# A dilated convolution on one core: the seventh pair's second image stored over 112 and four times 4 partitions, the last pair's first halves stored in one transfer

## The chip, the core and the metric

The kernel runs on one core of one Trainium2 chip. The metric is the device time of the program in microseconds; the lower the better. Three runs of the kernel before took 126.48, 126.51 and 126.69 us, the median is 126.51 us. One more execution was taken with the hardware profiler. It took 126.59 us, of which 124.8 us lie between the first and the last instruction (the span); all positions below are counted from the span's start.

## What is computed

A 3x3 convolution with dilation 2 and padding 2, in float32, of 16 images of 64 channels and 64x64 pixels into 16 images of 128 channels and 64x64 pixels:

```python
for b, co, ci, kh, kw:
    output[b, co] += weight[co, ci, kh, kw] * x_pad[b, ci, 2*kh:2*kh+64, 2*kw:2*kw+64]
```

The inputs are 16.8 MB of images and 0.3 MB of weights, the output is 33.6 MB. All of it crosses between HBM and SBUF once.

## The kernel before, in words

The 16 images are worked on as 8 pairs (`pb` 0 to 7). A pair's two images of 64 channels fill the 128 partitions of the input tile `x32`. A pair is cut into 4 groups of 16 image rows (`g` 0 to 3, `GR = 16`), so there are 32 groups `G`, written out in one Python loop. The instruction order on each engine is the order of the program text (`manual_schedule`).

For each group ScalarE casts the input to float16 (`cast`, line 73), VectorE adds neighbouring rows of it (`rowsum`, line 85), TensorE makes three PSUM tiles `psP`, `psA` and `psB` (line 171), ScalarE copies `psP` to SBUF (line 233), and VectorE adds it to `psA` and `psB` and writes the sums into the output tile `osb` (line 240). Casts run several groups ahead of the matmuls.

The output tile `osb` of a pair has 128 partitions (the output channels) of 8192 float32 each: 4096 of the pair's first image (16 KB), then 4096 of the second. There are three such tiles in rotation, and three of the float32 input tiles.

All transfers are issued by SyncE (SP), in program order: `load` (line 64) brings a pair's input in, `store` (line 185) takes one image's rows `r0` to `r1` of one output tile out, over the partition ranges in `rows`, and `store_both` (line 191) takes the same rows of both images in one transfer. Eight completion semaphores are used in turn, so a transfer is issued only after the one eight places before it has landed; a load also waits until its tile has been cast, and a store until VectorE has written what it reads. A DMA engine works through its share of the transfers in the order of their issue.

In the order of issue the part that matters here is: the load of pair 7 (`load(7, (0, 32, 64))`, two transfers of 32 rows, 8 KB a partition each), issued when pair 3 is done; then two stores of 2 MB for each of pairs 3 to 6, each image whole, 16 KB a partition. Pair 7 is the last. After its second group four transfers go out:

```python
store(pb, 0, 0, 2 * GR)                          # image 0, 32 rows, 8 KB a partition
store(pb, 1, 0, 2 * GR - ROWS4)                  # image 1, 24 rows, 6 KB a partition
store(pb, 1, 2 * GR - ROWS4, 2 * GR, FOUR)       # image 1, 8 rows: partitions 0-123, then 124-127
```

and after its fourth group the second halves, two transfers of 32 rows. The split at partition 124 matters because of how a transfer is shared out: in the trace a transfer over 128 partitions raises its completion semaphore sixteen times, once for each of the 16 DMA engines, and each engine has eight rows of it, whereas the transfer over 124 partitions raised it four times from engines, and the packet records show four engines with 31 rows of 2 KB each; the transfer over the last 4 partitions gave the same four engines one row each.

Of the kernel before, what the change touches and what calls it, by code (L numbers as in the profile page):

```python
# [10 lines left out]
def kernel(  # L11
# [9 lines left out]
    B, CI, H, W = x.shape  # L21
# [7 lines left out]
    P = 128  # L29
# [6 lines left out]
    GR = 16  # L36
# [3 lines left out]
    npairs = B // 2  # L40
    ngroups = npairs * NG
    chunk_rows = [(g * GR + (d if g else 0), min((g + 1) * GR + d, H)) for g in range(NG)]
    XF = 3
# [17 lines left out]
    def load(pb, cuts=(0, H)):  # L61
        x32_tiles[pb] = fpool.tile([P, HW], f32, tag="x32", name="x32")
        for lo, hi in zip(cuts[:-1], cuts[1:]):
            nc.sync.dma_start(  # L64
                out=x32_tiles[pb][:, lo * W : hi * W], in_=x_pair[pb, :, lo * W : hi * W]
            )
# [10 lines left out]
    def rowsum(c):  # L77
        pb, g = divmod(c, NG)
        if g == 0:
            xs_tiles[pb] = sxpool.tile([P, HW // 2], f16, tag="xs", name="xs")  # L80
        v = x16_tiles[pb][:, g * GR * W : (g + 1) * GR * W].rearrange(
            "p (b e q) -> p b e q", e=2, q=2 * W
        )
        s = xs_tiles[pb][:, g * NH : (g + 1) * NH].rearrange("p (b q) -> p b q", q=2 * W)
        nc.vector.tensor_tensor(out=s, in0=v[:, :, 0], in1=v[:, :, 1], op=add)  # L85
# [67 lines left out]
    def casts(G):  # L153
        for n in range(2 if G else 3):
            c = ahead[0]
            if c >= ngroups or c > G + (7 if c < 2 * NG else 5):
                return
            cast(c)
            ahead[0] += 1

    def product(ps, src, kind, blk0, nblk, first, last):
        for j in (1, 0, 2):
            dw = (j - 1) * d
            o0, o1 = max(0, -dw), W - max(0, dw)
            t = kind * KW + j
            for hb in range(2):
                pp = slice(hb * CI, (hb + 1) * CI)
                rhs = src(pp, dw + o0, dw + o1)
                po = ps[:, hb * NH + blk0 * 2 * W : hb * NH + (blk0 + nblk) * 2 * W]
                po = po.rearrange("p (r w) -> p r w", w=W)[:, :, o0:o1]  # L170
                nc.tensor.matmul(  # L171
                    out=po,
                    lhsT=w_sb[pp, t * CO : (t + 1) * CO],
                    rhs=rhs,
                    start=first and j == 1,
                    stop=last and j == 2,
                )

    def blocks(x16, b0, n, e):
        v = x16.rearrange("p (b e r w) -> p b e r w", e=2, r=2, w=W)  # L180
        return lambda pp, c0, c1: v[pp, b0 : b0 + n, e, :, c0:c1]

    def store(pb, m, r0=0, r1=H, rows=((0, P),)):
        for lo, hi in rows:
            nc.sync.dma_start(
                out=out_img[2 * pb + m, lo:hi, r0 * W : r1 * W],
                in_=o_tiles[pb][lo:hi, m * HW + r0 * W : m * HW + r1 * W],
            )

    def store_both(pb, r0, r1):  # L190
        nc.sync.dma_start(
            out=out_img[2 * pb : 2 * pb + 2, :, r0 * W : r1 * W].rearrange("m o q -> o m q"),
            in_=o_tiles[pb].rearrange("p (m q) -> p m q", m=2)[:, :, r0 * W : r1 * W],
        )

    FOUR = ((0, P - 4), (P - 4, P))
    ROWS4 = 8

    for G in range(ngroups):
        pb, g = divmod(G, NG)  # L200
        x16 = x16_tiles[pb]
        xs = xs_tiles[pb].rearrange("p (r w) -> p r w", w=W)
        if g == 0:
            o_tiles[pb] = opool.tile([P, 2 * HW], f32, tag="osb", name="osb")
        o = o_tiles[pb].rearrange("p (m b e q) -> p m b e q", m=2, e=2, q=2 * W)
        b0 = g * NBLK

        def summed():
            ps = ppool.tile([P, 2 * NH], f32, tag="p", name="psP")
            sv = lambda pp, c0, c1: xs[pp, g * GR // 2 : (g + 1) * GR // 2, c0:c1]  # L210
            product(ps, sv, 0, 0, NBLK, True, True)
            return ps

        if G:
            psP = summed()

        psA = apool.tile([P, 2 * NH], f32, tag="ab", name="psA")
        product(psA, blocks(x16, b0, NBLK, 1), 1, 0, NBLK, True, False)
        z = 1 if g == 0 else 0
        product(psA, blocks(x16, b0 + z - 1, NBLK - z, 1), 2, z, NBLK - z, False, True)  # L220

        psB = apool.tile([P, 2 * NH], f32, tag="ab", name="psB")
        product(psB, blocks(x16, b0, NBLK, 0), 3, 0, NBLK, True, False)
        z = 1 if g == NG - 1 else 0
        product(psB, blocks(x16, b0 + 1, NBLK - z, 0), 4, 0, NBLK - z, False, True)

        if not G:
            psP = summed()

        if not G:  # L230
            casts(0)
        p_sb = spool.tile([P, 2 * NH], f32, tag="psb", name="p_sb")
        nc.scalar.copy(out=p_sb, in_=psP)  # L233
        if G:
            casts(G)
        if G + 1 < ngroups:
            rowsum(G + 1)
        pv = p_sb.rearrange("p (m b q) -> p m b q", m=2, q=2 * W)
        for e, ps in ((0, psA), (1, psB)):
            nc.vector.tensor_tensor(  # L240
                out=o[:, :, b0 : b0 + NBLK, e],
                in0=ps.rearrange("p (m b q) -> p m b q", m=2, q=2 * W),
                in1=pv,
                op=add,
            )

        if G == 0:
            load(XF)
        if g == NG - 1 and 0 < pb < npairs - XF - 1:
            load(pb + XF + 1, (0, H) if pb < 3 else (0, H // 2, H))  # L250
        if G == NG - 2:
            store(0, 0, 0, (NG - 1) * GR)
            store(0, 1, 0, (NG - 1) * GR)
        if G == NG - 1:
            store_both(0, (NG - 1) * GR, H)
            load(XF + 1)
        elif pb == npairs - 1:
            if g % 2 == 1:
                store(pb, 0, (g - 1) * GR, (g + 1) * GR)
                if g == 1:  # L260
                    store(pb, 1, 0, 2 * GR - ROWS4)
                    store(pb, 1, 2 * GR - ROWS4, 2 * GR, FOUR)
                else:
                    store(pb, 1, (g - 1) * GR, (g + 1) * GR)
        elif g == NG - 1:
            store(pb, 0)
            store(pb, 1)

# [34 lines left out]
```

## Time and profile before

| what | value |
|---|---|
| median of three runs | 126.51 us (126.48 to 126.69) |
| profiled execution | 126.59 us |
| its span | 124.8 us |
| TensorE busy | 105.2 us, 84% of the span |
| VectorE busy | 91.0 us, 73% |
| ScalarE busy | 64.9 us, 52% |
| DMA moved | 50.78 MB, mean 407 GB/s |
| last VectorE instruction ends | 109.5 us |
| last store issued | 109.94 us |
| last store landed | 123.98 us |

A busy TensorE row counts pipelined matmuls, so 84% is not a distance to its peak. The DMA row counts the share of time in which the 16 DMA engines had a packet; packets of one engine overlap by 3 or 4 ns in the records, so that a wholly busy engine shows 1.01 to 1.02. The position of each packet, its duration and its size stand in the trace's packet records, and the moments at which a transfer's semaphore was raised in its semaphore records.

### The profile page before, as it was taken

To read this page: it belongs to the slowest core of one execution; us is meant where nothing else is said; L and a number is where in the kernel's file an instruction comes from. 1 tells how busy PE (TensorE), PEld (TensorE's weight loads), DVE (VectorE), ACT (ScalarE), POOL (GpSimd) and SP (SyncE) were. 2 spreads that over 40 slices of the span, in tenths; PEclk is the share of its full clock that TensorE was granted. 3 is DMA by queue.
4 is the path that set the end of the run, shared out by engine and by line. 5 is a ranking of instruction groups with operands and counts; after the bars stand their busy time and mean duration, and the time that the engine had idled before them with its cause. 6 is when DMAs were issued, how large, how long until landed. Compare 5 with 4: busy or idle time off the path is not lost.

```text
span 124.8 us, 2343 instructions
## 1 busy us (share of the span) xinstructions
PE 105.2 (84%) x1002; PEld 56.9 (46%) x1002; DVE 91.0 (73%) x103; ACT 64.9 (52%) x68; POOL 2.3 (2%) x8
## 2 busy tenths in 40 slices
PE   6985999999999999999999999999999999600000
PEld 2342555555555555555555555555555555300000
DVE  0661998988898889888988898889888988700000
ACT  4368897665666566656665666566653333200000
POOL 2400000000000000000000000000000000000000
PEclk9999999999999999999999999999999999965555
DMA  5999999999999999999999999999999999999981
GB/s 142 356 437 446 431 420 441 360 429 402 457 432 425 425 415 436 438 431 399 420 441 412 415 441 431 441 420 425 431 425 425 425 436 431 431 412 414 428 374 74
DMA packets 4594, 50.78 MB, mean 407 GB/s; under 512 B 488, under 2 KB 488, under 8 KB 1256
## 3 DMA queue, kind: packets, MB, share of 16 engines
q1 hardware_dynamic: 4584, 50.63, 96.5%
q8 instruction: 8, 0.13, 0.4%
q14 instruction: 2, 0.02, 0.0%
HBM read 17.07 MB, written 33.55 MB: 406 GB/s over the span
## 4 chain that ended last, share of the span: by engine, by line
PE 76%; DMA 6%; ACT 2%; DVE 1%; DVEq 1%; SPq 1%; issue 0%
PE psA L171 31%; PE psB L171 30%; PE psP L171 16%; DMA x<-in_x_dram 6%; ACT x L73 2%; DVE osb L240 1%; DVEq L300 1%; ACT p_sb L233 1%; SPq L64 0%; SPq L88 0%; DVEq L240 0%
## 5 line engine op out<-in xcount | busy, mean ns | idle before, releaser
L171 PEld LDWEIGHTS <-w_sb 64*128 64x128 f16 x960 | 54.6, 94 | 46.4 <-issue 1.6
L233 ACT COPY p_sb<-psP 128x1024 f32<-128x1024 f32 x32 | 32.4, 1013 | 36.8 <-issue 21.5
L240 DVE TENSOR_TENSOR osb<-psA,p_sb 128x1024 f32<-128x1024 f32 x32 | 39.2, 1225 | 13.5 <-PE psA L171 9.8
L171 PE MATMUL psA<-x,w_sb 64*128 64x496 f16 (+3 forms) x384 | 45.1, 365 | 0.5 <-ACT x L146 0.5
L171 PE MATMUL psB<-x,w_sb 64*128 64x496 f16 (+3 forms) x384 | 45.1, 365 | 0.0
L240 DVE TENSOR_TENSOR osb<-psB,p_sb 128x1024 f32<-128x1024 f32 x32 | 39.1, 1222 | 0.0
L73 ACT CAST x<-x 128x1024 f16<-128x1024 f32 (+2 forms) x31 | 32.1, 1045 | 0.6 <-DMA x<-in_x_dram 0.6
L171 PE MATMUL psP<-xs,w_sb 64*128 64x496 f16 (+1 forms) x192 | 26.0, 371 | 1.3 <-ACT p_sb L233 1.3
L85 DVE TENSOR_TENSOR xs<-x 128x512 f16<-128x512 f16 x32 | 13.3, 416 | 0.7 <-ACT x L73 0.7
L101 PE MATMUL dm<-zero 128*128 128x512 f16 x12 | 4.9, 539 | 1.2 <-DVE zero L93 1.2
L101 PEld LDWEIGHTS <-zero 128*128 128x128 f16 x12 | 1.3, 126 | 3.1 <-issue 1.7
L111 DVE CAST wd<-w 128x192 f16<-128x192 f32 x1 | 0.5, 505 | 2.4 <-DMA w<-in_weight_dram 2.4
L113 ACT ACT_TABLE_LOAD x1 | 1.3, 1283 | 0.7 <-PEq L286 0.7
L124 PEld LDWEIGHTS <-wd 128*64 128x64 f16 x30 | 0.9, 109 | 1.4 <-DVE wd L111 0.7
L124 PE MATMUL wt<-ident,wd 128*64 128x128 f16 x30 | 1.4, 224 | 0.0
L136 ACT CAST w_sb<-wt 128x384 f16<-128x384 f32 x1 | 0.5, 480 | 1.7 <-PE wt L124 1.7
L113 ACT CAST wd<-w 128x192 f16<-128x192 f32 x1 | 0.5, 542 | 1.5 <-DMA w<-in_weight_dram 1.5
L146 ACT CAST x<-x 128x512 f16<-128x512 f32 x1 | 0.6, 620 | 0.6 <-DMA x<-in_x_dram 0.6
L93 DVE MEMSET zero<- 128x256 uint32 x1 | 0.3, 272 | 0.9 <-PEq L286 0.9
L138 DVE CAST w_sb<-wt 128x384 f16<-128x384 f32 x1 | 0.6, 558 | 0.4 <-PE wt L124 0.4
L112 POOL TENSOR_TENSOR wd<-w 128x192 f16<-128x192 f32 x1 | 0.8, 797 | 2.3 <-DMA w<-in_weight_dram 2.3
L115 POOL CAST wd<-w 128x192 f16<-128x192 f32 x1 | 0.8, 810 | 0.0
(11 smaller groups left out, 3.8 us busy)
## 6 DMA issues: line engine op xcount, KB each, us to landing
out_dram<-osb SPq DMA_DIRECT2D x12, 2048.0 KB, 18.1
x<-in_x_dram SPq DMA_DIRECT2D x6, 2048.0 KB, 14.8
out_dram<-osb SPq DMA_DIRECT2D x4, 1024.0 KB, 13.1
out_dram<-osb SPq DMA_DIRECT2D x2, 1536.0 KB, 11.3
x<-in_x_dram SPq DMA_DIRECT2D x2, 1024.0 KB, 19.0
x<-in_x_dram SPq DMA_DIRECT2D x1, 1088.0 KB, 5.7
x<-in_x_dram SPq DMA_DIRECT2D x1, 960.0 KB, 7.5
out_dram<-osb SPq DMA_DIRECT2D x1, 768.0 KB, 15.2
```

What stands on the lines that cost most here:

```text
L73: nc.scalar.copy(out=x16_tiles[pb][:, lo * W : hi * W], in_=x32_tiles[pb][:, lo * W : hi * W])
L85: nc.vector.tensor_tensor(out=s, in0=v[:, :, 0], in1=v[:, :, 1], op=add)
L101: nc.tensor.matmul(out=dm[:, 0:512], lhsT=zero[:, 0:P], rhs=zero)
L112: nc.gpsimd.tensor_tensor(out=wdv[:, 3], in0=wv[:, 0], in1=wv[:, 1], op=sub)
L113: nc.scalar.copy(out=wdv[:, 2], in_=wv[:, 0])
L115: nc.gpsimd.tensor_copy(out=wdv[:, 4], in_=wv[:, 2])
L124: nc.tensor.matmul(out=wts[k % 3][r * CI : (r + 1) * CI, c0 + j * CO : c0 + (j + 1) * CO], lhsT=wd[:, t * CI : (t + 1) * CI], rhs=ident,)
L138: nc.vector.tensor_copy(out=t2[0], in_=t2[1])
L171: nc.tensor.matmul(out=po, lhsT=w_sb[pp, t * CO : (t + 1) * CO], rhs=rhs, start=first and j == 1, stop=last and j == 2,)
L233: nc.scalar.copy(out=p_sb, in_=psP)
L240: nc.vector.tensor_tensor(out=o[:, :, b0 : b0 + NBLK, e], in0=ps.rearrange("p (m b q) -> p m b q", m=2, q=2 * W), in1=pv, op=add,)
L300: with _tile.TileContext(nc) as tc:
```

## The change

Three edits, all of transfers that SP issues:

- The load of pair 7 is one transfer of 2 MB, 16 KB a partition, as the other pairs' loads are; it was two of 1 MB.
- The second image of pair 6 was stored in one transfer over 128 partitions; it is now stored in five: one over partitions 0 to 111 and four over 4 partitions each (112-115 to 124-127), rows of 16 KB in all of them.
- The first halves of pair 7's two images were stored in four transfers (32 rows of image 0; 24 rows of image 1; 8 rows of image 1 over 124 and over 4 partitions). They are now stored by one transfer of both images, with two runs of 8 KB for each partition.

The second halves of pair 7 are stored as before. No instruction of TensorE, VectorE, ScalarE or GpSimd is added, removed or moved. SP issues 32 transfers in all, as before.

```diff
-    FOUR = ((0, P - 4), (P - 4, P))
-    ROWS4 = 8
+    LOW = P - 16
+    FOURS = ((0, LOW),) + tuple((lo, lo + 4) for lo in range(LOW, P, 4))
...
-            load(pb + XF + 1, (0, H) if pb < 3 else (0, H // 2, H))
+            load(pb + XF + 1)
...
-            if g % 2 == 1:
-                store(pb, 0, (g - 1) * GR, (g + 1) * GR)
-                if g == 1:
-                    store(pb, 1, 0, 2 * GR - ROWS4)
-                    store(pb, 1, 2 * GR - ROWS4, 2 * GR, FOUR)
-                else:
-                    store(pb, 1, (g - 1) * GR, (g + 1) * GR)
+            if g == 1:
+                store_both(pb, 0, 2 * GR)
+            elif g == 3:
+                store(pb, 0, 2 * GR, H)
+                store(pb, 1, 2 * GR, H)
         elif g == NG - 1:
             store(pb, 0)
-            store(pb, 1)
+            store(pb, 1, rows=FOURS if pb == npairs - 2 else ((0, P),))
```

## The prediction

> **What bounds the kernel now.** I read the page's slices and queues first, then what SP waits for, then the last microseconds in narrow stretches, then SP's and ScalarE's order of time. On the page:
>
> ```profile
> DVE  0661998988898889888988898889888988700000
> DMA  5999999999999999999999999999999999999981
> q1 hardware_dynamic: 4584, 50.63, 96.5%
> q8 instruction: 8, 0.13, 0.4%
> ```
>
> The DMA row is full from the second slice to the last but one, while VectorE, the last engine to work, stops at 109.5 us. The page's chain ends on compute and does not follow the DMA, so its 76% of TensorE is not what sets the end. SP's waits after 100 us say what does:
>
> ```profile
> SPq L300 <- DMA out_dram<-osb: 13.0, 3, 8.3
> ```
>
> At the end of the program SP waits 13 us for stores alone. Whether the engines have work throughout is read in stretches (columns: stretch, its length, granted clock, DMA share, GB/s):
>
> ```profile
> 60.00:72.00 12.00, 1.00 1.01 427
> ...
> 96.00:108.00 12.00, 1.00 1.01 430
> 108.00:120.00 12.00, 0.59 1.00 419
> 120.00:124.80 4.80, 0.50 0.39 164
> ```
>
> A share of 1.01 is all sixteen engines without a gap. The packet records agree: nearly every packet starts 3 or 4 ns before the one before it on its engine ends. So the kernel is bound by the DMA engines, each with its own list of packets, and its end is the end of the engine that finishes last. How unevenly they finish, in stretches as long as one 8 KB packet takes:
>
> ```profile
> 119.98:120.29 0.31, 0.50 0.95 402
> 120.59:120.90 0.31, 0.50 0.76 321
> 121.20:121.51 0.31, 0.50 0.58 241
> 121.82:122.12 0.31, 0.50 0.51 214
> 122.43:122.73 0.31, 0.50 0.26 107
> 122.73:123.04 0.31, 0.50 0.25 107
> 123.04:123.35 0.31, 0.50 0.13 54
> ```
>
> One engine is 27 GB/s: fifteen are at work at 120.1, nine at 121.4, four at 122.9; in the last row two packets start, and the later one ends last. Following the packets back engine by engine, the last ends are 123.65, 123.35, 123.29 and 123.26. The first two of these four are engines that had the 2 KB rows (of which the other two end at 122.50 and 122.58); call the latest of these **d**. The ends at 123.29 and 123.26 are two other engines, call them the **slow pair**; the remaining ten end between 120.05 and 122.2. Landing is seen 0.33 us behind d's last packet (123.98), and the span ends 0.8 us later.
>
> **The change part by part.** The price of a packet is its duration less the overlap, from the packet records: 16 KB 611 - 4 = 607 ns, 8 KB 309 - 3 = 306, 6 KB 234 - 3.5 = 230.5, 2 KB 84 - 4 = 80, and 9 - 3 = 6 for the 4-byte packet that raises a semaphore.
>
> How 112 rows are shared out, no row shows. 128 rows went to sixteen engines, 124 and 4 rows to four; each time the number of engines divides the rows. 112 is 16 x 7, so I take sixteen engines with seven rows each; the far end, four engines as with 124 rows, is a rival below.
>
> The four engines that d belongs to, before: load of pair 7 16 x 306 = 4896; second image of pair 6 8 x 607 = 4856; then 8 x 306 = 2448, 8 x 230.5 = 1844 and 32 x 80 = 2560; together 16604 ns and 7 semaphore packets. After: load 8 x 607 = 4856; pair 6 (7 + 4) x 607 = 6677; both first halves 16 x 306 = 4896; together 16429 ns and again 7 semaphore packets. Saved: **175 ns**. In bytes nothing moves: they had 62 + 2 KB of small rows for a fair share of 16 KB, 48 KB too many; now they have 4 x 16 KB less the one row of 16 KB that they lose, 48 KB too many again. The gain is only that 64 KB travel in 4 packets for 32.
>
> The other twelve, the slow pair among them, before: 4896 + 4856 + 2448 + 1844 = 14044 and 5 semaphore packets; after: 4856 + 7 x 607 + 4896 = 14001 and 3. Saved: 43 + 12 = **55 ns**.
>
> So d ends at 123.65 - 0.175 = 123.47, the slow pair at 123.29 - 0.055 = 123.23: d still ends last, and the gain is d's 0.175 us. Were d quicker still, the slow pair would cap the gain at 123.65 - 123.23 = 0.42 us.
>
> What is costed at nothing, and its cover:
>
> ```profile
> 55.09 1.20 SPq L64 DMA_DIRECT2D x<-in_x_dram  x2
> 97.17 0.97 SPq L185 DMA_DIRECT2D out_dram<-osb  x2
> 103.27 2.34 SPq L185 DMA_DIRECT2D out_dram<-osb  x4
> 109.54 1.03 SPq L185 DMA_DIRECT2D out_dram<-osb  x2
> 82.03 1.16 ACT L73 CAST x<-x 128x1152 f16<-128x1152 f32 x1
> ```
>
> The whole load lets pair 7's first cast (82.03 us, the last row, from ScalarE's timeline) wait for all of it; the two halves had landed at 73.04 and 75.49, so 6.5 us of cover are left. Four more issues behind 97.17, at 0.6 us each (2.34 / 4), end by 101, before the next store can be issued at 103.27; three issues fewer there leave SP idle, which costs nothing. An issue also waits for the transfer eight places before it. The places move between the load of pair 7 and the small stores; the tightest is now the very last store, which comes to stand behind the first image of pair 6 (landed 109.67, while this store was issued at 109.94). The four small ones stand behind stores of pairs 3 and 4, landed by 95.0. The earliest engine would run dry only at some 115 us (its end 120.05 less two shares of 2.45), 5 us behind the last issue. VectorE's wait for the store of pair 3, 0.3 us at 85.4, is covered likewise, since VectorE is 14 us ahead of the end.
>
> [...]
>
> **The sum.** Against the profiled execution's own time: 126.59 - 0.175 = 126.42 us. That execution stood 0.08 us above the median of 126.51, so on the median 126.34 us, 0.14% less. A measurement of this kernel tells about 0.2%, 0.25 us, from no change.
>
> **The rivals.**
>
> *The instruction fetches fall on other engines.* The eight packets of q8 are 16 KB each, one about every 13 us, each on another engine, which they hold back by one packet, 607 ns. In the packet records the one at 81.04 fell on d and those at 16.11 and 95.10 on the slow pair: three of the four latest engines have had one each. If another list of transfers moves them, d ends at 122.87 and the slow pair sets 123.23: -0.42, 126.09 us. If one falls on the other late engine of the four (123.35), it ends at 123.35 - 0.175 + 0.607 = 123.78, +0.13: 126.64. Against it: the instructions fetched are TensorE's and they don't change, and the three runs lie within 0.21 us, so in the kernel before the places seem to be fixed.
>
> *The four engines get in each other's way* (slower). In each 4-row transfer four engines read four neighbouring partitions in packets of 607 ns. d's neighbours run 0.3 us and about 1.1 us ahead of it, so half of each of its packets overlaps the next engine's. If two such readers halve each other's rate, d's four packets grow by up to 0.3 us each: +1.2 - 0.175, 127.5 us. It decides over the forecast from 44 ns a packet on, where the gain is used up. Against it: the 2 KB rows, read by four engines beside twelve others, took 84 ns every single time. But those were 31 partitions apart, and the four neighbouring rows of the old kernel hardly met: they were 84 ns long and started at 117.52, 117.59, 118.36 and 118.66.
>
> *Small transfers hold their engines.* If each of the four must land before its engine goes on (0.33 us as at the end), d gains 4 x 0.33 = 1.3 us: 127.7. Against it: behind the 124-row transfer the next row started at once, at 117.516 behind a semaphore packet at 117.510. [...]
>
> *The 112 rows are not spread over sixteen engines.* Over four: 28 rows each for 7, 21 x 607 = 12.7 us, 139 us. Over fourteen with eight rows each, as every engine has of 128: d has one row more, +0.61 - 0.175 = +0.43, 126.94 us.
>
> **How the numbers follow.** The forecast, 126.34, has 0.62: with the scatter of the runs (0.1 each way) and the engines' stalls on the early loads its own range is 126.15 to 126.55; 0.13 of it lies below 126.26, which is 0.25 under the median, 0.47 within, 0.02 above. The fetches moved: 0.22, of which 0.17 faster, 0.03 within and 0.02 slower by over 0.2%. Neighbours in the way 0.09, small transfers held 0.03, 112 rows otherwise 0.04: all slower. Faster 0.13 + 0.17 = 0.30; within 0.2% 0.47 + 0.03 = 0.50; slower 0.02 + 0.02 + 0.16 = 0.20. The range runs from the fetches' best, 126.09, with a little scatter, to 126.75, which takes in the fetches' worst and a tenth of scatter; left out are the three slower rivals, 0.16.
>
> **What the profile after would show.** Packets of 112 rows on sixteen engines, 7 each, and 16 KB packets of 611 ns in the four small transfers; if these take 650 or more, neighbours are in the way. The 2 KB and 6 KB packets gone. The last packet's end at 123.47 on one of the four engines. The same eight fetches on the same engines; d without one would show as an end set by two engines that had no small transfers. DMA share 1.01 until 120. I am wrong if the last stretches show one or more of the four engines alone for over half a microsecond, or if a load's stalls, which set the engines apart by up to 1 us in the first 25 us, come out otherwise.

## The result, and the profile after

The changed kernel is slower: ratio 1.0229 to the kernel before, 95% interval 1.0202 to 1.0255. Its six runs took 129.15 to 133.91 us (median 132.6), the kernel before 126.48 to 126.90 in as many (median 126.59); the ratio is formed from the two quickest, 129.15 and 129.8, since runs far above a kernel's fastest are left out as disturbed, but here the spread came with the change, and by the medians it is 4.7% slower. The profiled execution is one of the long ones, 133.82 us with a span of 132.0; sizes read from it are its own.

On the page of the kernel after, the slices and the queues:

```profile
DVE  0562998988888898889888988888898872000000
DMA  5999999999999999999999999999999999999410
GB/s 153 384 442 447 422 432 396 419 433 422 429 442 342 437 417 434 432 417 437 427 429 422 437 432 427 422 432 427 427 422 437 432 417 323 325 375 387 181 52 15
...
q1 hardware_dynamic: 4304, 50.63, 92.7%
q8 instruction: 8, 0.13, 0.4%
```

The bytes are the same, the packets fewer, as the sum had it. VectorE stops 0.4 us later than it did, at 109.9 us. But in the 34th and 35th slice (from 109 us) the engines are still full and move a quarter less. In stretches (columns: stretch, its length, granted clock, DMA share, GB/s), the kernel after:

```profile
104.00:108.00 4.00, 1.00 1.02 426
108.00:110.00 2.00, 1.00 1.04 369
110.00:112.00 2.00, 1.00 0.99 324
112.00:114.00 2.00, 0.73 1.00 324
114.00:116.00 2.00, 0.50 1.00 336
...
122.00:124.00 2.00, 0.50 0.53 225
124.00:126.00 2.00, 0.50 0.27 115
...
130.00:132.00 2.00, 0.50 0.02 8
```

and the kernel before:

```profile
108.00:110.00 2.00, 1.00 0.99 418
110.00:112.00 2.00, 0.55 0.95 406
112.00:114.00 2.00, 0.50 0.97 412
114.00:116.00 2.00, 0.50 1.02 427
```

A share of 1.00 at 324 GB/s is read as slow packets: no engine waits for work, packets take longer. The packet records say which. Behind 105 us, 37 of 177 packets of 16 KB took over 1.2 times 611 ns, up to 2459, and 19 of the 8 KB packets that travelled beside them over 1.2 times 309; together 31.5 us too long over sixteen engines (in all packets of both sizes, instruction fetches left out). In the kernel before the same count is one packet and 0.6 us. The stretch begins with the 112-row transfer. The DMA issues of the two kernels from 98 us on, that of the five-part store after and of one whole image before:

```profile
out_dram<-osb SPq DMA_DIRECT2D x1, 1792.0 KB, 23.5
out_dram<-osb SPq DMA_DIRECT2D x4, 64.0 KB
```

```profile
out_dram<-osb SPq DMA_DIRECT2D x1, 2048.0 KB, 17.0
```

The 112 rows land 23.5 us after their issue, although they are an eighth less than the image that took 17.0. Their semaphore was raised by sixteen engines, the first at 110.84 and the last at 121.42 us. Of the four small transfers the quickest engine made each in 0.61 us, and the last raises of the four lie 0.6, 1.6 and 1.8 us apart. As the engines come out of this stretch more than 10 us apart, the tail is long: one engine alone works from about 128 to 131 us.

This last engine is none of the four. An engine comes to its four small rows behind its share of the 112, and the small rows had all landed by 118.02, so the engine that raised the semaphore of the 112 rows at 121.42 had no small ones. It had finished the store before at 110.32 at the latest; its seven rows took 11.1 us or more where the price of 607 ns asks for 4.25.

### The profile page after: what moved, and what is told of

It reads as the page before. It is cut to its first block, busy times and chain, and to the rows that moved or that the text cites. A ratio compares the mean times of both kernels' runs of the same rounds, so it can differ in the third digit from the quotient of the medians.

```text
span 132.0 us, 2342 instructions
## 1 busy us (share of the span) xinstructions
PE 106.3 (80%) x1002; PEld 56.8 (43%) x1002; DVE 91.1 (69%) x103; ACT 64.9 (49%) x68; POOL 2.2 (2%) x8
## 3 DMA queue, kind: packets, MB, share of 16 engines
q1 hardware_dynamic: 4304, 50.63, 92.7%
## 4 chain that ended last, share of the span: by engine, by line
PE 80%; DVE 1%; DVEq 1%; ACT 1%; issue 0%
PE psA L171 30%; PE psB L171 29%; PE psP L171 16%; PE dm L101 4%; PE wt L124 1%; DVE osb L240 1%; DVEq L298 1%; ACT p_sb L233 1%; DVE zero L93 0%; DVEq L240 0%
## 5 line engine op out<-in xcount | busy, mean ns | idle before, releaser
L101 PE MATMUL dm<-zero 128*128 128x512 f16 x12 | 5.5, 593 | 1.2 <-DVE zero L93 1.2
L124 PE MATMUL wt<-ident,wd 128*64 128x128 f16 x30 | 1.9, 277 | 0.0
L138 DVE CAST w_sb<-wt 128x384 f16<-128x384 f32 x1 | 0.6, 558 | 1.2 <-PE wt L124 1.2
L134 DVE CAST w_sb<-wt 128x384 f16<-128x384 f32 x1 | 0.6, 558 | 0.5 <-PE wt L124 0.5
## 6 DMA issues: line engine op xcount, KB each, us to landing
out_dram<-osb SPq DMA_DIRECT2D x1, 1792.0 KB, 23.5
```

The lines of the kernel that those rows point to most:

```text
L101: nc.tensor.matmul(out=dm[:, 0:512], lhsT=zero[:, 0:P], rhs=zero)
L124: nc.tensor.matmul(out=wts[k % 3][r * CI : (r + 1) * CI, c0 + j * CO : c0 + (j + 1) * CO], lhsT=wd[:, t * CI : (t + 1) * CI], rhs=ident,)
L134: nc.vector.tensor_copy(out=t0[0], in_=t0[1])
```

## The experiments

The theory after this profile, a supposition for the runs to test: packets are slow because several engines at once read partitions that share a way out of SBUF, which the 112-row transfer and the four-row ones bring about and a transfer over 128 does not. The rivals: the store of both images in one transfer or the single load; the addresses written in HBM; small transfers as such. Where one time is given without an interval, the kernel was run once, under the profiler.

**The five-part store undone.** The rest of the change stays.

```diff
-            store(pb, 1, rows=FOURS if pb == npairs - 2 else ((0, P),))
+            store(pb, 1)
```

> The changed kernel with the second image of pair 6 stored in one transfer over 128 partitions again; the single load of pair 7 and the single transfer of the first halves stay. If the five-part store is the cause (112 rows or the four small ones): no packet behind 100 us over some 650 ns, every engine has its fair share, the slow pair ends one 16 KB row later than forecast (123.23 + 0.61 = 123.84) and the time is 126.59 + 0.19 = 126.8 us. If the store of both images in one transfer or the single load is the cause: it stays at 129 us or more with packets of 1 to 2 us.

Measured: ratio 1.0066 (1.0043 to 1.0088), median 127.36 us. Not one 8 KB packet behind 105 us is over 309 ns, and one of 16 KB is over 1.2 times 611 (1006, beside an instruction fetch). The rate is back, in the same stretches of this run:

```profile
108.00:112.00 4.00, 1.00 1.00 422
112.00:116.00 4.00, 0.61 0.99 418
```

So the loss is the five-part store's. The 0.66% that remain are more than the 0.2 us expected; the run without small rows, below, takes that up.

**Its parts by themselves.** First the 112 rows alone, then the four small transfers alone.

```diff
-    FOURS = ((0, LOW),) + tuple((lo, lo + 4) for lo in range(LOW, P, 4))
+    FOURS = ((0, LOW),)
```

> The changed kernel without the four 4-row transfers: partitions 112 to 127 of that image are left out. If the 112-row transfer slows its own packets: 16 KB packets of 1 to 2.5 us remain between 106 and 120 us and the time stays at 128 us or more. If the four small transfers do it: all packets at 611 ns, the slow pair ends last at 123.23, 126.4 us.

```diff
-    FOURS = ((0, LOW),) + tuple((lo, lo + 4) for lo in range(LOW, P, 4))
+    FOURS = tuple((lo, lo + 4) for lo in range(LOW, P, 4))
```

> The changed kernel without the 112-row transfer: partitions 0 to 111 of that image are left out, the four 4-row transfers stay. Seven rows of 607 ns less on each engine: 126.42 - 4.25 = 122.2 us with all packets at 611 ns, if the 112-row transfer alone is the cause. If four engines that read four neighbouring partitions slow each other: their 16 KB packets take 1.2 to 2.4 us, and the time is 123.4 us or more.

Measured: 130.49 us for the 112 rows alone, 28 of 167 packets of 16 KB over 1.2 times their time, up to 1819 ns; 128.15 us for the four small ones alone, 13 of 66 over it, up to 2820 ns, 16 KB packets being few there. Both parts collide, each without the other: some 4 us for the first (130.49 against the forecast 126.4) and some 6 for the second (128.15 against 122.2). The two do not add up to the change's loss. With the small ones alone, one of the four engines is the last; in the complete kernel the last engine is another, which the 112 rows had held up.

**Two halves.**

```diff
-    FOURS = ((0, LOW),) + tuple((lo, lo + 4) for lo in range(LOW, P, 4))
+    FOURS = ((0, P // 2), (P // 2, P))
```

> The changed kernel with that image in two transfers of 64 partitions each, in place of the five: the same bytes on each engine as in one transfer of 128. If packets are slow because two engines read partitions that share a way out of SBUF (which 64 neighbouring partitions would do for every engine), 16 KB packets take about 1.2 us there and the time is 126.8 + 8 x 0.6 = 131.6 us. If it is the addresses in HBM, or the odd share of seven rows, all packets stay at 611 ns and the time is 126.8 us.

Measured: 132.41 us. The rate in the stretches:

```profile
108.00:112.00 4.00, 1.00 1.00 309
112.00:116.00 4.00, 0.51 0.94 287
```

57 of 182 packets of 16 KB are over 1.2 times their time, and between 110.7 and 113.2 us many of them take 1.21 to 1.28 us, twice 611 ns; the longest took 2934. Here every engine has its fair share and every transfer goes to sixteen engines, so neither an odd share nor a low count of engines is needed: two transfers of 64 neighbouring partitions are enough. That 64 neighbouring partitions would make every engine share a way out was supposed; what is measured is the 57 packets and the 132.41 us.

**Reads or writes.** Only four small transfers, from partitions four apart (0, 4, 8 and 12 plus r; the other 112 partitions of the image are left out); then the same places in HBM, read from neighbouring partitions.

```diff
-            store(pb, 1, rows=FOURS if pb == npairs - 2 else ((0, P),))
+            if pb == npairs - 2:
+                for r in range(4):
+                    nc.sync.dma_start(
+                        out=out_img[2 * pb + 1, r:16:4, :], in_=o_tiles[pb][r:16:4, HW:]
+                    )
+            else:
+                store(pb, 1)
```

> [...] If reading neighbouring partitions is what slowed them: all packets at 611 ns and about 122.7 us. If small transfers as such, or four engines with 16 KB rows, are slow: packets of 1.5 to 2.8 us again and 128 us.

```diff
-                        out=out_img[2 * pb + 1, r:16:4, :], in_=o_tiles[pb][r:16:4, HW:]
+                        out=out_img[2 * pb + 1, r:16:4, :], in_=o_tiles[pb][LOW + 4 * r : LOW + 4 * r + 4, HW:]
```

> As the run with four partitions apart, and with its destinations in HBM (rows 0, 4, 8, 12 plus r of the image), but read from four neighbouring partitions (112 to 127, so the rows hold other channels' data, and the rest is left out). If the reads from SBUF collide: packets of 1.5 to 2.8 us and about 128 us, as with neighbouring rows in HBM. If the addresses written in HBM decide: 611 ns and 122.7 us.

Measured: 122.77 us and 127.98 us. The stretches of the first and then of the second:

```profile
104.00:108.00 4.00, 1.00 1.01 424
108.00:112.00 4.00, 1.00 0.98 416
112.00:116.00 4.00, 0.69 1.00 424
```

```profile
104.00:108.00 4.00, 1.00 1.01 389
108.00:112.00 4.00, 0.96 0.99 360
112.00:116.00 4.00, 0.50 0.97 393
```

With partitions four apart no 16 KB packet of the stores is over 672 ns; with neighbouring ones, written to the very same places, 15 of 65 are over 1.2 times their time, up to 2673 ns. So four small transfers with 16 KB rows were no hindrance here as such; the reads from SBUF decide, 122.77 us against 127.98. This is the pair of runs that settles it for the small transfers. For the 112 rows and the halves no run separates reads from writes; that the same holds there is carried over from here.

What the neighbouring partitions share, and how far such a group of them reaches, no run shows.

**More engines on fewer partitions.**

```diff
-    FOURS = ((0, LOW),) + tuple((lo, lo + 4) for lo in range(LOW, P, 4))
+    FOURS = tuple((lo, lo + 16) for lo in range(0, P, 16))
```

> The changed kernel with that image in eight transfers of 16 neighbouring partitions, one row of 16 KB for each engine. If four neighbouring partitions share a way out of SBUF: four engines on each, 16 KB packets of up to 4 x 607 = 2.43 us, and at worst 8 x 1.82 = 14.6 us more than in one transfer, 142 us; as the engines drift apart and spread over eight ways rather than four, less, but over 131.6. If the share is by engines of a transfer alone, or by 64 partitions: no worse than the two halves, 132.4 us.

Measured: 131.43 us, no worse than the halves. Single packets go to 2.9 us, but the excess behind 105 us, 45.7 us over sixteen engines, is little more than the halves' 40.1, and the engines finish closer together: the last store's semaphore is raised between 123.73 and 128.58 us, in the halves between 122.90 and 129.51. The engines are 3.5 us apart already when they finish the first of the eight transfers (raises from 106.97 to 110.45), so four of them seldom read one transfer's rows at the same time; that this kept the worst case of 142 us away is an inference. The run does not tell the theory from the rival that 64 partitions are what counts.

**The size of the packets.** My strongest evidence against collisions had been the 2 KB rows of the kernel before, all at 84 ns.

```diff
-    FOURS = ((0, LOW),) + tuple((lo, lo + 4) for lo in range(LOW, P, 4))
+    HALVES = ((0, P // 2), (P // 2, P))
...
-            store(pb, 1, rows=FOURS if pb == npairs - 2 else ((0, P),))
+            if pb == npairs - 2:
+                store(pb, 1, 0, 32, HALVES)
+                store(pb, 1, 32, 48, HALVES)
+                store(pb, 1, 48, 56, HALVES)
+                store(pb, 1, 56, 64)
+            else:
+                store(pb, 1)
```

> The changed kernel with pair 6's second image cut by image rows: 32 rows (8 KB a partition), 16 rows (4 KB) and 8 rows (2 KB), each in two transfers of 64 partitions, and the last 8 rows (2 KB) over 128 partitions. [...] If sharing costs by bytes: packets of 8, 4 and 2 KB all take about twice 309, 159 and 84 ns, the store takes 4.9 x 7/8 = 4.3 us more than in one transfer, 131.6 us. If small packets escape it: 8 KB packets at 620, 2 KB packets at 84, and some 2.4 to 3.7 us more, 129.8 to 131.

Measured: 130.19 us. Over 1.2 times their time behind 105 us: 21 of the 128 packets of 4 KB (excess 3.6 us) and 15 of the 256 of 2 KB (1.9 us; half of these 256 belong to the last transfer, over 128 partitions), the longest 2 KB packet at 352 ns. Of the 640 packets of 8 KB, 27 are over it, up to 1239 ns. So small packets are not exempt, but few are hit. The other way round, the form of the kernel before with 8 KB rows:

```diff
-    FOURS = ((0, LOW),) + tuple((lo, lo + 4) for lo in range(LOW, P, 4))
+    FOUR = ((0, P - 4), (P - 4, P))
...
-            store(pb, 1, rows=FOURS if pb == npairs - 2 else ((0, P),))
+            if pb == npairs - 2:
+                store(pb, 1, 0, H // 2)
+                store(pb, 1, H // 2, H, FOUR)
+            else:
+                store(pb, 1)
```

> The changed kernel with the second half of pair 6's second image in rows of 8 KB over 124 partitions and over 4, as the kernel before stores its 2 KB rows; the first half over 128. Four engines have 32 rows of 306 ns for a fair share of 8, +7.3 us, so about 126.59 + 5.5 = 132 us if nothing collides: then 124 partitions over four engines are free of collisions whatever the row's size. If they were free only because the rows were of 2 KB: 8 KB packets of 400 to 620 ns on the four engines and on those whose partitions they read, and 134 us or more.

Measured: 137.40 us, 5 us over what the bytes on four engines ask for, with 48 of 768 packets of 8 KB over 1.2 times their time, up to 1186 ns, and an excess of 15.4 us. So the form "124 and 4 partitions" is not free of collisions as such; only its 2 KB rows went without them, all 128 at 84 ns.

**The whole kernel with the small transfers that did not collide by themselves.**

```diff
-            store(pb, 1, rows=FOURS if pb == npairs - 2 else ((0, P),))
+            store(pb, 1, rows=((16, P),) if pb == npairs - 2 else ((0, P),))
+            if pb == npairs - 2:
+                for r in range(4):
+                    nc.sync.dma_start(
+                        out=out_img[2 * pb + 1, r:16:4, :], in_=o_tiles[pb][r:16:4, HW:]
+                    )
```

> The changed kernel, complete, with the 112-row transfer over partitions 16 to 127 and the four small ones over partitions 0, 4, 8, 12 plus r, which were free of collisions by themselves. The shares of the engines are those of the change. If both parts of the five-part store cost time: the small ones no more, the 112 rows as in the run without the small ones (130.5, some 4 us over what its bytes ask for), so 129 to 131 us with 16 KB packets of up to 2 us in the 112 rows. If the small transfers did nearly all of it: 126.3 to 127 us. If the 112 rows did all of it: no better than the change, 129 to 134.

Measured: 128.83, 129.04, 131.96 and 132.46 us. The lowest is close to the change's lowest, 129.15, and the spread is nearly as wide, so in the complete kernel the 112 rows bring most of the loss, and most of the spread; the middle of the four, 130.5, for the change's 132.6 leaves something to the small ones, but with four and six runs so far apart that share is not settled. The stretches of the 128.83 us run:

```profile
108.00:112.00 4.00, 0.83 0.98 340
112.00:116.00 4.00, 0.50 0.96 358
```

Its excess is 22.4 us, that of the change's 133.82 us run 31.5. Its last engine again is none of the four: the last semaphore of the 112 rows is raised at 116.33, the last of the small ones at 115.28.

**What the shares are worth.** First the kernel before without its small rows, then with seven image rows in them instead of eight.

```diff
-                if g == 1:
-                    store(pb, 1, 0, 2 * GR - ROWS4)
-                    store(pb, 1, 2 * GR - ROWS4, 2 * GR, FOUR)
-                else:
-                    store(pb, 1, (g - 1) * GR, (g + 1) * GR)
+                store(pb, 1, (g - 1) * GR, (g + 1) * GR)
```

> The kernel before, with the first half of the last pair's second image in one transfer over 128 partitions: no small rows, every engine its fair share, two loads of 1 MB and two stores of the first halves kept. The slow pair gets 16 KB more, 0.62 us, and ends last at 123.29 + 0.62 = 123.91 against 123.65: +0.26, 0.2% slower. The run with the five-part store undone has the same share and came out 0.7% slower: if its 0.4 beyond the share is due to the single load or to the store of both images, this run stays at +0.2%; if the share is worth more than the one profile showed, it too is 0.5 to 0.7% slower.

```diff
-    ROWS4 = 8
+    ROWS4 = 7
```

> The kernel before, with 7 image rows instead of 8 in the two small transfers (124 and 4 partitions). By the engines' ends of before: the four engines are relieved by 6 KB each, 0.23 us, d ends at 123.42; the others get 2 KB more, the slow pair ends at 123.37. So 0.23 us less than before, 0.18%. If the load of the four engines does not set the end, no change or 0.07 more.

Measured: 1.0044 (1.0027 to 1.0062) without the small rows, 0.9996 (0.9979 to 1.0012) with seven. The share that the small rows shift is worth 0.4%, about twice what one profile had given; the five-part store undone, with the same shares, is at 0.66% with an interval that overlaps this one, so the single load and the store of both images are left with little. With seven rows no gain is seen; the 0.18% expected lie at the very edge of the interval.

## Why the prediction was wrong

*What bounds the kernel.* Right: the engines' lists of packets set the end, before and after, and the last engine sets the time (its last packet ended at 123.65 and at 130.87 us, the spans at 124.8 and 132.0). Wrong: that d, one of the four, ends last. After the change the last engine is one that had no small transfer, in the profiled run and in that of the small transfers four apart, with 112 rows beside them.

*The count of engines.* Right: the 112-row transfer ran on sixteen engines, and the four small ones on four each, by the count of their semaphores' raises; the rival with fewer engines falls.

*The bytes and packets of each engine.* Right as a count, 4304 packets for 4584 and the same bytes. But the sum's price, 607 ns for each 16 KB packet of the 112 rows and of the small transfers, is the step that failed. That price came from transfers over 128 partitions. Behind 105 us the packets are 31.5 us too long in all, 2 us an engine in the mean, up to 2459 ns in one packet; the last engine's seven rows alone took at least 6.8 us more than 7 x 607 ns. So the forecast end of 123.47 us became 130.87 in the profiled run, where 0.175 us were to be gained.

*The rival "the four engines get in each other's way".* This was the mechanism, with 0.09. Three things were wrong with it. Its place was too narrow: I looked for neighbours in the four small transfers alone and took the 112 rows as harmless because sixteen engines with even shares had them. Yet with seven rows an engine in place of eight, an engine may read partitions that another reads in a transfer of 128. From which partition a packet comes no record tells, so that this slowed the 112 rows is an inference, with the halves behind it. And its dismissal rested on the 2 KB rows, which "took 84 ns every single time": true, and no evidence for 16 KB, as the same form with 8 KB rows showed. I had even noted that the neighbouring rows of the old kernel hardly met. That its 2 KB rows were 31 partitions apart was my estimate from the 31 rows of each engine; which partitions they were was not shown. The price given, doubling where two readers meet, is what many packets of the halves showed (1.21 to 1.28 us); but single packets went to 2.5 us after the change and 2.8 with the small transfers alone, so the rival's 127.5 us was too low as well.

*The rival "small transfers hold their engines".* Refuted by the four transfers with partitions four apart: 122.77 us against 122.7 expected, no 16 KB packet of the stores over 672 ns.

*Instruction fetches.* Eight again, each within 1.8 us of its place before (first 15.98, last 109.55 us; before 16.11 and 107.83). Whether they fell on the same engines the records do not tell, nor whose instructions they bring; the spacing, 244 to 272 of TensorE's instructions from one fetch to the next in the kernel before, fits TensorE's. They play no part in the loss: the run with the five-part store undone has the same eight. But their price, one packet of 607 ns, was read too low. In the kernel before the fetch at 95.09 us took 939 ns, the packet behind it 1006, and the next began at 97.02, so that engine lost 1.3 us; over the eight it is 1.3 to 1.4 us, twice the price.

*What was costed at nothing.* The single load, the issues and the waits stayed covered: pair 7's first cast began at 82.41 us for 82.03, and the five issues of the store were out by 99.9 us. The very last issue was not quick; it took 2.96 us for 0.62 (the last two issues of SP's order of time together 3.38 for 1.03), but its first packets were not due before 118 us, when the first engine was through with the store ahead of it.

```profile
109.92 3.38 SPq L185 DMA_DIRECT2D out_dram<-osb  x2
```

## What to carry to other kernels

Take a packet's price from the partitions that it is to be used for: 16 KB took 611 ns over 128 partitions, and many took 1210 to 1280 in the halves of 64. Cut a store by columns or image rows and keep all 128 partitions, as the run with the five-part store undone did (no 8 KB packet over 309 ns); if a few engines must get more, give them partitions four apart (0, 4, 8, 12 plus r is the only set tried; by themselves no packet over 672 ns), or rows of 2 KB in the form of the kernel before (84 ns each), and look for a full DMA share at a falling rate: here 1.00 at 324 GB/s was the sign of engines in each other's way. Even shares and a full count of engines did not exclude it in the halves (57 of 182 packets slow), and the 84 ns of the 2 KB packets did not carry over to 8 KB (48 of 768 slow in the same form).

## What the runs showed of the hardware that I had not expected

- Two transfers over 64 neighbouring partitions each doubled the time of many of their packets although all sixteen engines took part (611 to 1210-1280 ns), and the transfers beside them were slow too (8 KB packets of the next store at up to 641 ns).
- With collisions the time was erratic: 129.15 to 133.91 us after the change and 128.83 to 132.46 with the small transfers four apart. The kernel before and the other three that were run more than once stay within 1.2 us, but for one run of the kernel before at 128.93. I take it that it depends on how far the engines stand apart when they come to that store; that was not tried.
- Why the 2 KB rows of the kernel before escape entirely, all 128 at 84 ns, when 15 of 256 packets of 2 KB were slow in the run cut by image rows, stays open; so does why only 48 of 768 packets of 8 KB were slow in the form of the kernel before.
- SP's issue of the last store took longer in two runs with slow packets: 2.96 us after the change for 0.62 before, 2.90 with neighbouring partitions for 0.43 with partitions four apart. Why was not tried.
